# A two-group hybrid layer step on one core: features on partitions from the output projection on, the last projection as seven block products, and eight modulation columns moved into the gates

## The chip, the cores and the metric

The kernel runs on one core of one Trainium2 chip. The metric is the device time of one execution in microseconds, taken as the median of several runs. Beside it stand profiles: one execution each, recorded by the hardware profiler, in which every instruction has a start, a length and the instruction or DMA that released it. Engine names are those of the profile: PE (TensorE matmuls), PEld (its weight loads), DVE (VectorE), ACT (ScalarE), POOL (GpSimd) and SP (SyncE, which here only issues DMAs).

## The reference

One layer (DEPTH is 1) is applied to two groups of tokens: 512 sample tokens and 128 prompt tokens, 640 together, with 1024 features. Each group has its own modulation vector. The parts that the change touches are these:

```python
mod = jax.nn.silu(cvec) @ lw['w_ada'] + lw['b_ada']
sh1, sc1, g1, sh2, sc2, g2 = jnp.split(mod, 6, axis=-1)
h = rmsnorm(x, lw['norm1_g']) * (1.0 + sc1) + sh1
mix, ... = token_mixers(h, ...)          # ends: merged @ lw['w_o']
x = x + g1 * mix
h = rmsnorm(x, lw['norm2_g']) * (1.0 + sc2) + sh2
x = x + g2 * conv_ffn(h, ...)            # (silu(g) * a) @ w_down, 2816 hidden features
y = rmsnorm(x, final_norm_g)
```

`token_mixers` computes four branches from an input projection, a sigmoid gate for each branch, and `merged`, the gated sum of four branch projections. `conv_ffn` projects up to 2 x 2816 features, applies a three-tap convolution along the tokens, multiplies silu of one half by the other and projects down. Everything is fp32.

## The kernel before

**Arithmetic.** Each fp32 operand of a large product is split in two fp32r tiles, a high part (a copy, written by ACT) and a low part (the difference, written by DVE). A product is three matmul passes: high by high, high by low and low by high. Weights arrive in fp32 by DMA, issued by SP, and are split in the kernel, so every weight tile costs one copy on ACT and one subtraction on DVE. A few low parts are formed by a DMA on POOL's queue instead (`low_dma`).

**Stages, in the order of time.** Normalization, input projections and the mixers' own work (0 to about 285 us); the first gate's tiles, one after the other (285 to 355 us); the other gates as seven-product block pairs; the output projection `wo_tile` (544 to 601 us); the second normalization; the up projection, 22 pairs of hidden tiles, each pair as seven block products of 12 matmuls 128x320 per tile set (617 to 884 us); the down projection `down_tile` (869 to 1030 us); and the final normalization. In the middle stages features lie on partitions and the 640 tokens are the moving dimension, cut in two halves of 320. From the output projection on it is the other way: five tiles of 128 tokens are on partitions, and a matmul streams 512 output features.

**Output projection and second normalization.** `wo_tile` runs over two column halves and eight feature tiles. When a token tile is complete, DVE multiplies by the gate, which has been spread over partitions as a row (`gain_rows`, line 250, transposes it and a DMA broadcasts it), and adds x. `norm2` then squares with an accumulator on ACT, takes the power -0.5 on POOL (line 264), scales, turns the tile back with eight PE transposes (line 1229) and applies scale and shift (line 1240). High and low parts follow in pieces (line 1249). The matmuls of the first up products (line 1387, called the bridge below) are placed between the transposes; `operands` forms the sums and differences of the up projection's input blocks in two pieces, 192 and 128 tokens wide, while the bridge runs. The pair loop's matmuls are line 1392.

**Down projection.** For each half of 512 output columns there are 11 steps of two hidden tiles; a step has 30 matmuls 128x512, or in the second half 24 of 128x512 and 12 of 128x256 (line 1708). The activations come back from DRAM (`actd`). `down_out` (lines 1719 to 1740) multiplies by the gate row, adds x, squares, takes the power on POOL, scales on ACT and DVE, and stores. Eight modulation columns, numbers 40 to 47 (the gate g2), are computed beside this stage by `ada_cols`: each is a 512 KB load and, for each of the two groups, a multiplication with a summing output on DVE (line 223 before, 224 after).

**Order of the work.** A table of units is walked with loads four units ahead and preparation two ahead. Side work is written as generators; `start` puts one in, `tick` and `pe` advance a clock by estimated PE time, and a generator goes on when the clock has passed what it yielded. `drain` forces one to its end at that point. Within the sections where `fixed[0]` is true (the gate pairs, the up projection, and after the change the down projection), DVE, ACT and POOL follow the written order; DVE operations recorded by the helper have line 138 (137 after). Elsewhere, and on PE and SP, a list scheduler sets the order. Tiles live in regions with fixed tags (`region("X0", ...)`), so a tile's reuse waits for the readers of the one before.

## Time and profile before

| | |
|---|---|
| median of 3 runs | 1039.47 us (1039.32 to 1042.35) |
| profiled execution, its own time | 1039.43 us |
| its span, first to last instruction | 1037.7 us |
| PE busy | 1021.1 us, 98% of the span |
| DVE busy | 790.5 us, 76% |
| ACT busy | 520.6 us, 50% |
| POOL busy | 99.7 us, 10% |
| mean granted PE clock | 0.998 |

Matmuls are pipelined and overlap in the records, so the mean length of one is longer than the distance from one to the next; the distance is read from the chain of waits, where a stretch of matmuls stands with its count. An entry `[0.44 <-ACT MG L138]` behind a row says that the engine was idle 0.44 us before it and that ACT's writing of tile MG, recorded at line 138, ended the idle time. The profile's lines are shown where the prediction uses them.

### The profile page before, as it was taken

The numbers are of one execution on the slowest core, as the hardware profiler recorded it, in microseconds if no ns is written. First come the engines' busy times: TensorE is split into PE (matmuls) and PEld (weight loads), VectorE is DVE, ScalarE is ACT, GpSimd is POOL, SyncE is SP. The second block draws the span as 40 slices with busy tenths as digits, with TensorE's granted clock in tenths as the row PEclk, the third lists the DMA queues.
The fourth block names the chain that finished last, engine by engine and source line by source line (L and its number), as shares of the span: only waits on it lengthen the run. The fifth ranks groups of instructions, "written<-read, shape, count | busy, mean of one in ns | idle before, by whom it ended". The sixth has DMA issues, their size and how long they took to land. (4 is left out here: it accounts for less than half of the span.)

```text
span 1037.7 us, 18776 instructions
## 1 busy us (share of the span) xinstructions
PE 1021.1 (98%) x7648; PEld 962.1 (93%) x7648; DVE 790.5 (76%) x1271; ACT 520.6 (50%) x900; POOL 99.7 (10%) x145
## 2 busy tenths in 40 slices
PE   8999999999999999999999999999999999999997
PEld 6899989998899999999998898999999999888886
DVE  5658899789946567767768688998888887785734
ACT  6542353242333444444444377876777776632532
POOL 2000020211100000000000011211111121000201
PEclk9999999999999999999999999999999999999999
DMA  9854433544143122332178274666555569974212
GB/s 363 325 196 126 126 122 105 164 144 153 52 163 117 55 99 98 107 102 80 64 246 331 113 264 126 175 172 164 162 148 148 148 154 261 378 256 144 84 39 102
DMA packets 52759, 165.28 MB, mean 159 GB/s; under 512 B 7840, under 2 KB 14400, under 8 KB 49600
## 3 DMA queue, kind: packets, MB, share of 16 engines
q1 hardware_dynamic: 43424, 137.19, 38.7%
q0 software_dynamic: 9248, 26.89, 10.4%
q8 instruction: 60, 0.98, 0.4%
q14 instruction: 27, 0.22, 0.1%
HBM read 131.52 MB, written 21.52 MB: 147 GB/s over the span
## 5 line engine op out<-in xcount | busy, mean ns | idle before, releaser
L317 PE MATMUL g<-XH,w 128*128 128x320 f32 x832 | 200.0, 317 | 0.2 <-DVE MG L378 0.2
L317 PEld LDWEIGHTS g<-XH,w 128*128 128x128 f32 x832 | 141.9, 188 | 2.9 <-issue 2.0
L317 PE MATMUL g<-XL,w 128*128 128x320 f32 x416 | 129.0, 310 | 0.0
L317 PEld LDWEIGHTS g<-XL,w 128*128 128x128 f32 x416 | 78.3, 188 | 0.8 <-issue 0.5
L270 DVE TENSOR_TENSOR w<-raw,w 128x1024 fp32r<-128x1024 f32 x34 | 41.5, 1222 | 18.3 <-ACT w L269 17.6
L1708 PE MATMUL g<-w,XH 128*128 128x512 f32 (+1 forms) x216 | 47.5, 372 | 0.0
L269 ACT ACTIVATE w<-raw 128x1024 fp32r<-128x1024 f32 x34 | 35.8, 1052 | 20.9 <-PE g L1187 10.2
L1708 PEld LDWEIGHTS g<-w,XH 128*128 128x128 f32 x216 | 38.5, 188 | 7.6 <-ACT XH L1671 0.3
L1051 PE MATMUL m<-XH,w 128*128 128x320 f32 x192 | 45.0, 309 | 0.0
L138 DVE SCALAR_TENSOR_TENSOR X<-MG,p2t,X 128x641 f32<-128x641 f32 x44 | 38.9, 884 | 5.7 <-ACT X L138 4.8
L282 ACT ACTIVATE w<-raw 128x1024 fp32r<-128x1024 f32 (+1 forms) x26 | 29.4, 1130 | 22.3 <-PE g L317 9.5
L138 DVE SCALAR_TENSOR_TENSOR X<-X,p2t,X 128x641 f32<-128x641 f32 x44 | 38.9, 884 | 1.9 <-ACT X L138 1.0
L1708 PE MATMUL m<-w,XH 128*128 128x512 f32 (+1 forms) x180 | 40.2, 368 | 0.0
L1708 PE MATMUL g<-w,XL 128*128 128x512 f32 (+1 forms) x180 | 40.0, 373 | 0.0
L1392 PE MATMUL g<-XL,C 128*128 128x320 f32 x240 | 38.6, 310 | 0.4 <-ACT MG L138 0.4
L1392 PE MATMUL g<-XL,w 128*128 128x320 f32 x240 | 38.7, 310 | 0.0
L1708 PEld LDWEIGHTS g<-w,XL 128*128 128x128 f32 x180 | 32.2, 188 | 6.8 <-DVE dt L1719 0.6
L283 DVE TENSOR_TENSOR w<-raw,w 128x1024 fp32r<-128x1024 f32 (+1 forms) x26 | 33.9, 1302 | 4.2 <-ACT w L282 4.0
L1392 PEld LDWEIGHTS g<-XL,C 128*128 128x128 f32 x240 | 35.9, 188 | 1.1 <-ACT MG L138 1.1
L1392 PEld LDWEIGHTS g<-XL,w 128*128 128x128 f32 x240 | 36.0, 188 | 0.5 <-ACT MG L138 0.3
L1708 PEld LDWEIGHTS m<-w,XH 128*128 128x128 f32 x180 | 31.3, 189 | 5.3
L1708 PE MATMUL m<-w,XL 128*128 128x512 f32 (+1 forms) x150 | 33.2, 368 | 0.0
(541 smaller groups left out, 2701.2 us busy)
## 6 DMA issues: line engine op xcount, KB each, us to landing
raw<-in_w_up_dram SPq DMA_DIRECT2D x32, 512.0 KB, 4.9
raw<-in_w_gp_dram SPq DMA_DIRECT2D x18, 640.0 KB, 3.8
raw<-in_w_down_dram SPq DMA_DIRECT2D x22, 512.0 KB, 4.0
raw<-in_w_in_dram SPq DMA_DIRECT2D x19, 512.0 KB, 4.0
H<-in_w_adt_dram SPq DMA_DIRECT2D x16, 512.0 KB, 4.2
actd<-X POOLq DMA_DIRECT2D x22, 320.5 KB, 5.3
X<-in_w_adt_dram SPq DMA_DIRECT2D x10, 512.0 KB, 4.0
raw<-in_w_gate_dram SPq DMA_DIRECT2D x8, 640.0 KB, 3.9
```

The source lines that it names most:

```text
L138: r = f(*args, **kw)
L269: act(w[0], raw, AF.Copy)
L270: vec.tensor_tensor(w[1], raw, w[0].bitcast(F32), ALU.subtract)
L282: act(w[:, 0], raw, AF.Copy)
L283: low = lambda: vec.tensor_tensor(w[:, 1], raw, w[:, 0].bitcast(F32), ALU.subtract)
L317: mm(o, w[:, h, k0 + k, :], r(k)[:, s], start=(k == 0 and i == 0), stop=(k == kt - 1 and i == 2))
L1051: mm(o, w[:, k, :], x[:, k, :], start=(first and k == 0 and j == 0), stop=(k == 3 and j == 2), skip_group_check=True)
L1392: mm(o, w[:, k, :], x[:, k, :], start=(first and k == 0 and j == 0), stop=(k == 3 and j == 2), skip_group_check=True)
L1708: mm(acc[nh][t + c0 // 256][:, 0:c1 - c0], sl[k][hx][:, t * P:(t + 1) * P], w[:, hw, k, c0:c1], start=(kk_ == 0 and k == 0 and i == 0), st ...
```

## The change

1. **Features on partitions to the end.** x is kept transposed (`x_t`, a new input layout). The output projection has eight column blocks of 128 features by two token halves of 320: 384 matmuls 128x320 (`wo_mm`). The gate is now a scalar per partition (`add_out`). The second normalization squares on ACT, adds the squares of the eight feature tiles on DVE, sums over partitions by a product with ones (`stats_a`), takes the power for three token blocks on POOL, and spreads the result over partitions by a second product (`stats_c`). The 40 transposes and the gate rows go. `operands` forms all nine sums, differences and low parts at the full width of 320, behind the statistics of the second token half.
2. **Down projection as seven block products.** The 22 hidden tiles are cut in two halves of 11, the output columns in two halves of 512 and the tokens in two halves of 320. Products run in the order 1, 5, 6, 4, 7, 2, 3, each in six groups of two hidden tiles (the last of one), 924 matmuls 128x320 in all (`group_mm`, line 1797). Sums of weight blocks are formed in place by accumulating DMAs on POOL's queue, sums and differences of activations by DVE (`prep_x`). `ended` adds a product's four outputs to x. One token half is normalized in place with features on partitions; the other is turned by 24 transposes (line 1834) and normalized with tokens on partitions. The two output halves are put together on the host.
3. **Columns 40 to 47 in the gates.** `ada_cols` for them is started when the first branch's input projections end, and is drained at the fifth tile of the first gate.

The core of the diff:

```diff
@@ ada_cols, gate_tile
+                start(ada_cols(range(40, 48), None, col_home, HD[4]))
+        if (bi, n) == (0, 4):
+            drain(lambda: "ada47" in R)
-        start(ada_cols(range(40, 48), "MG1", lambda f: region("H", [P, D]) if f % 2 else down_home(), 5))
@@ output projection
+    def add_out(ps, n, c, g, eng=None):
+        x = x2s(n, c)
+        for (t0, t1, v) in pieces(c):
+            (eng or vec).scalar_tensor_tensor(x[:, t0:t1], ps[:, t0:t1], gcol[:, g, v, n % 8:n % 8 + 1], x[:, t0:t1],
+                                              ALU.mult, ALU.add)
...
+    def stats_a(c, m):
+        for j, t in enumerate((0, P, HC - P)):
+            mm(m[:, 2 * j:2 * j + 2], axs[0][:, c, t:t + P], ones[:, 0:2], start=True, stop=True)
...
+    def stats_c(dg, m):
+        for j, (t, w) in enumerate(((0, P), (P, P), (2 * P, HC - 2 * P))):
+            mm(m[:, t:t + w], onesf, dg[:, j, P - w:P], start=True, stop=True)
...
+    def wo_mm(o, w, c, ks, first, last):
+        for k in ks:
+            for i, (hw, hx) in enumerate(((0, 0), (0, 1), (1, 0))):
+                mm(o, w[:, hw, k, :], mh[k // 2][:, hx, k % 2, c * HC:(c + 1) * HC],
+                   start=(first and k == ks[0] and i == 0), stop=(last and k == ks[-1] and i == 2))
+            tick(0.44)
@@ up_all, operands
+            if p_ == 0:
+                stats_a(1, g[0][:, 1])
+                dg = stats_b(1, g[0][:, 1])
+            if p_ == 1:
+                stats_c(dg, g[1][:, 1])
+                for q in range(2):
+                    normed(1, q, g[1][:, 1])
+                shifted(1, 0, False)
+                shifted(1, 1, True)
...
+        operands()
@@ down projection
+    def prep_w(i):
+        p_, g = GR[i]
+        n = many(g)
+        wr = slots.pop(("raw", i)) if p_ in (2, 3) else chain(g)
+        w = slots["w", i] = wp.tile([P, 2, 2, 512], F32R, tag="w", name=nm("w"))
+        oact(w[:, 0, 0:n], wr, AF.Copy)
+        ovec.tensor_tensor(w[:, 1, 0:n], wr, w[:, 0, 0:n].bitcast(F32), ALU.subtract)
+        if p_ in CHAIN:
+            opool.dma_start(flat2(wr), flat2(wblock(CHAIN[p_], g)), accum_op=ALU.add)
...
+    def prep_x(i):
...
+        if p_ == 5:
+            ovec.tensor_tensor(x, a21, a22, ALU.subtract)
+            ovec.tensor_tensor(a21, a11, a21, ALU.subtract)
+        elif p_ == 6:
+            ovec.scalar_tensor_tensor(x, a21, -1.0, a22, ALU.mult, ALU.subtract)
+        elif p_ == 7:
+            ovec.tensor_tensor(a22, a22, a21, ALU.add)
+        elif p_ == 3:
+            ovec.tensor_tensor(a12, a12, a22, ALU.subtract)
...
+    def group_mm(o, i, js):
+        for kk in range(many(g)):
+            k = 2 * g + kk
+            for j in js:
+                for q, (h, x) in enumerate(((0, 0), (0, 1), (1, 0))):
+                    mm(o[j], w[:, h, kk, j * P:(j + 1) * P], s[:, x, kk, :], ...)
```

Three places show how the order moves. In the rows, a name is tile, buffer number and version; the shape is the output's.

DVE at the start of the up projection, before: `X0` and `XL1` hold the normalized blocks, `X1` the sums, `B`, `A`, `D` the operands' high and low parts.

```order
L1249 TENSOR_TENSOR XL0_557_6178<-X0_566_6274,XL0_557_6178 128x4x128
L138 TENSOR_TENSOR X1_591_6511<-X0_566_6274 128x4x192
L138 TENSOR_TENSOR X1_591_6511<-X1_591_6511,XL1_559_6180 128x4x192
L138 TENSOR_TENSOR X0_566_6274<-XL1_559_6180,X0_566_6274 128x4x192
L138 TENSOR_TENSOR X1_591_6511<-X0_566_6274 128x4x128
L138 TENSOR_TENSOR MG1_585_6453<-m_587_6463,s1_590_6508 128x320
L1249 TENSOR_TENSOR XL0_557_6178<-X0_566_6274,XL0_557_6178 128x4x128
L138 TENSOR_TENSOR B_593_6513<-X1_591_6511,B_593_6513 128x4x192
L138 TENSOR_TENSOR A_592_6512<-X1_591_6511,A_592_6512 128x4x192
```

The same place after the change, from the scaling by the second half's statistics (`X1` by the broadcast in `g`) to the pair's weight lows:

```order
L137 TENSOR_TENSOR X1_578_6343<-X1_578_6343,g_602_6587 128x1280
...
L137 TENSOR_TENSOR X0_616_6738<-X1_578_6343 128x1280
L137 TENSOR_TENSOR X0_616_6738<-X0_616_6738,XL1_577_6337 128x1280
L137 TENSOR_TENSOR B_619_6741<-X0_616_6738,B_619_6741 128x1280
L137 TENSOR_TENSOR X1_578_6343<-XL1_577_6337,X1_578_6343 128x1280
L137 TENSOR_TENSOR A_618_6740<-X0_616_6738,A_618_6740 128x1280
L137 TENSOR_TENSOR D_620_6742<-X1_578_6343,D_620_6742 128x1280
L137 TENSOR_TENSOR X0_616_6738<-XL1_577_6337,X0_616_6738 128x1280
L137 TENSOR_TENSOR XL0_617_6739<-X1_578_6343,XL0_617_6739 128x1280
L137 TENSOR_TENSOR XL1_621_6755<-X0_616_6738,XL1_621_6755 128x1280
L137 TENSOR_TENSOR MG1_606_6622<-m_612_6685,s1_613_6698 128x320
L137 TENSOR_TENSOR w_624_6788<-F_600_6581,w_624_6788 128x1024
```

Two pieces of 192 and 128 have become one operation each, and the first of them stands behind the scaling by the second half's statistics; the pair's weight lows are last.

DVE in the first gate's tiles, before: MG0 are the merges, the 128x1280 rows the operands of the block pairs.

```order
L915 TENSOR_TENSOR MG0_324_3529<-g_342_3716,gt_341_3714 128x640
L965 TENSOR_TENSOR C_336_3647<-B_337_3648,C_336_3647 128x1280
L283 TENSOR_TENSOR w_346_3734<-raw_328_3554,w_346_3734 128x1280
L967 TENSOR_TENSOR C_336_3647<-C_336_3647 128x1280
L977 TENSOR_TENSOR X0_343_3723<-C_336_3647,X0_343_3723 128x1280
```

After, the stretch ahead of the fifth merge (MG1):

```order
L224 SCALAR_TENSOR_TENSOR junk_365_3857,ar_366_3858<-MG1_315_3431,S0_89_1054 128x1024
...
L224 SCALAR_TENSOR_TENSOR MG1_315_3431,ar_366_3858<-MG1_315_3431,S0_89_1054 128x1024
L962 TENSOR_TENSOR X0_370_3903<-C_342_3662,X0_370_3903 128x1280
...
L224 SCALAR_TENSOR_TENSOR junk_368_3897,ar_369_3898<-MG1_315_3431,S0_89_1054 128x1024
L962 TENSOR_TENSOR F_372_3905<-B_343_3663,F_372_3905 128x1280
L224 SCALAR_TENSOR_TENSOR MG1_315_3431,ar_369_3898<-MG1_315_3431,S0_89_1054 128x1024
...
L905 TENSOR_TENSOR MG1_373_3907<-g_374_3908,gt_367_3895 128x640
```

The sixteen column operations stand between the merges and the operands' operations, the last one just ahead of the fifth merge, whose tile takes over the region of the columns' data.

PE where the down projection begins, after the change: `g_780` is the up projection's last pair, `m_796` to `m_799` the four output blocks of the first product.

```order
L1437 MATMUL g_780_9288<-D_620_6742,w_779_9253 128x320
L1797 MATMUL m_796_9479<-XH_788_9411,w_787_9407 128x320
...
L1797 MATMUL m_798_9481<-XH_788_9411,w_787_9407 128x320 x2
L1437 MATMUL g_780_9288<-XL0_617_6739,w_779_9253 128x320 x12
...
L1797 MATMUL m_799_9482<-XH_788_9411,w_787_9407 128x320 x3
L1437 MATMUL g_780_9288<-XL1_621_6755,w_779_9253 128x320 x12
L1797 MATMUL m_796_9479<-XH_788_9411,w_789_9422 128x320 x3
...
L1797 MATMUL m_796_9479<-XH_788_9411,w_802_9509 128x320
```

The first group (weights `w_787`) now stands around the last pair's two last products, the second group directly behind; `w_802` is the fourth group's.

More of the change, by code (lines that the diff above doesn't have):

```diff
@@ L953, in g_operands @@
         yield 8
+        while "ada47" not in R:
+            yield 1
         (a11, a12), (a21, a22) = [[x[:, h] for h in range(2)] for x in f]
@@ L1253, in tile_step, with pieces @@
[L1253 to L1257 removed]
+    st2 = const.tile([P, 4, 4], F32, name="st2")
+    axs = [None]
+    x2d = dram.tile([2, P, 4, T], F32, name="x2d")
+    KO = ((0, 1, 4, 5), (2, 3, 6, 7))
+    HOLD = 5
+    def pieces(c):
+        return ((0, HC, 0),) if c == 0 else ((0, TS - HC, 0), (TS - HC, HC, 1))
@@ new lines, in normed, with shifted @@
+    def normed(c, q, m):
+        f = hh[c][:, q]
+        ovec.tensor_tensor(f, f, m[:, 0:HC].unsqueeze(1).to_broadcast([P, 4, HC]), ALU.mult)
+    def shifted(c, q, on_vec):
+        f = hh[c][:, q]
+        for k in range(4):
+            for (t0, t1, v) in pieces(c):
+                x, sh = f[:, k, t0:t1], modt[:, 24 + 4 * q + k, v:v + 1]
+                if on_vec:
+                    ovec.tensor_scalar(x, x, sh, None, ALU.add)
+                else:
+                    oact(x, x, AF.Identity, bias=sh)
@@ L1261, in tile_step @@
+    for n in range(8):
+        plain(lambda n=n: feat(a["w_o"][n]), lambda w, n=n: wo_tile(n, w))
     actd = dram.tile([NPAIR, P, T + 1], F32, name="actd")
@@ L1556, in up_pair @@
             prod(b1, p_, 7, False)
[L1558 to L1571 removed]
+        if p_ == NPAIR - 1:
+            down_start(1)
@@ new lines, in backs, with chain, wblock @@
+    def backs(o, h, c, eng=nc.sync):
+        k = 0
+        while k < 11:
+            k1 = min(11, k + 8 - (12 * o + k) % 8)
+            back(o, h, c, k, k1, eng)
+            k = k1
+    def chain(g):
+        tag, n, at = (("S0", 4, 2 * g), ("S0", 4, 2 * g), ("H", 2, 0), ("F", 5, 0), ("F", 5, 2), ("F", 5, 4))[g]
+        if "w" + tag not in dn:
+            dn["w" + tag] = region(tag, [P, n, 512])
+        return dn["w" + tag][:, at:at + many(g)]
+    def wblock(b, g):
+        return a["w_down"][b[0], b[1]][:, 2 * g:2 * g + many(g)]
```

663 lines of the change are left out of this document (363 added, 300 removed).

## The prediction

> **What bounds the kernel now.** I read the page's busy shares and slices first, for what is busy in every stage.
>
> ```profile
> PE 1021.1 (98%) x7648; PEld 962.1 (93%) x7648; DVE 790.5 (76%) x1271; ACT 520.6 (50%) x900; POOL 99.7 (10%) x145
> PE   8999999999999999999999999999999999999997
> PEclk9999999999999999999999999999999999999999
> ```
>
> TensorE is busy in 98% of the span at the full granted clock. So the time is a sum of matmul pitches plus a few stalls, and a change is worth what it takes out of, or puts between, matmuls. The pitches stand in the chain of waits (start us, length, what); a stretch without a stall divided by its count gives one pitch.
>
> ```profile
> 668.91 10.56 PE g L1392 x72
> ...
> 904.89 1.36 PE m L1708 x6
> 906.25 5.44 PE g L1708 x24
> ...
> 972.18 2.07 PE g L1708 x12
> 974.25 4.83 PE m L1708 x24
> ```
>
> A 128x320 matmul takes 10.56/72 = 0.1467 us, a 128x512 one 5.44/24 = 0.2267. A down-projection step of 30 takes 6.80; the steps of the second half, with 256-wide pieces, 6.90. Next, the busy time by stage (busy us and instructions of PE, PEld, DVE, ACT, POOL; clock; DMA share; GB/s): gates' first tiles (two rows), up projection, its hand-over to the down projection, both down halves, and the end.
>
> ```profile
> 284.00:327.00 43.00, 42.88 (x301) 40.34 (x300) 28.34 (x38) 18.04 (x22) 0.00 (x0) 1.00 0.44 150
> 327.00:336.00 9.00, 9.00 (x63) 9.00 (x62) 2.32 (x2) 2.07 (x2) 0.00 (x0) 1.00 0.27 89
> 632.00:870.00 238.00, 238.00 (x1620) 237.53 (x1619) 213.84 (x315) 172.69 (x296) 43.67 (x58) 1.00 0.61 162
> 870.00:893.00 23.00, 23.00 (x122) 19.71 (x121) 17.98 (x24) 14.93 (x24) 3.12 (x5) 1.00 1.03 345
> 893.00:950.00 57.00, 57.00 (x254) 47.10 (x253) 45.19 (x69) 23.08 (x29) 0.00 (x0) 1.00 0.73 248
> 950.00:1030.00 80.00, 80.00 (x414) 68.32 (x412) 42.53 (x58) 28.45 (x48) 10.14 (x9) 1.00 0.23 79
> 1030.00:1038.00 8.00, 0.13 (x2) 0.00 (x0) 1.92 (x6) 1.69 (x6) 0.55 (x1) 0.68 0.32 132
> ```
>
> VectorE has little room in the up projection (213.84 of 238) and no stall comes of it there; it has most room in the second down half. The only stalls that this change touches are behind the output projection, in the timeline of PE (the bracket is the idle time before the row and its releaser):
>
> ```profile
> 616.75 0.31 PE L1392 MATMUL g<-B,E 128*128 128x320 f32 x1
> ...
> 625.57 1.59 PE L1392 MATMUL g<-A,w 128*128 128x320 f32 x9 [1.15 <-DVE w L138]
> ...
> 631.36 1.92 PE L1392 MATMUL g<-B,w 128*128 128x320 f32 x12
> ```
>
> From 616.75 to 631.36 72 matmuls run; at the pitch they need 10.56 us, so 4.05 us are lost there.
>
> **The change part by part.** The profiled execution takes 1039.43 us for a span of 1037.7; that is the median of the runs, 1039.47, within 0.04, so I add the terms to 1039.4.
>
> *Down projection.* Before: 11 x 6.80 + 11 x 6.90 = 150.7 us. After: 6 groups a product, five of 24 and one of 12 matmuls, so 132 x 7 = 924 of 128x320, 135.5 us. Term: **-15.2**, if PE stays the bound. The Trainium skill (TensorE: Matmul & The Clock Gate, "Back-to-back issue gap") gives a warm gap of N/2.4 + 2.5 ns, so 135.8 and 215.8 ns; by it the term would be 924 x 0.1358 - (594 x 0.2158 + 132 x 0.1092) = -17.1. The trace has 10.8 ns more in every matmul, which tells against a change to more and narrower ones, and its pitch stands.
>
> *Does VectorE keep up there?* Prices:
>
> ```profile
> L138 DVE TENSOR_TENSOR w<-raw,w 128x1024 fp32r<-128x1024 f32 x15 | 18.3, 1222 | 2.7 <-ACT w L138 2.7
> L138 DVE TENSOR_TENSOR MG<-MG,ga 128x640 f32<-128x640 f32 x12 | 9.9, 825 | 0.4
> L138 DVE TENSOR_TENSOR gb<-m,gb 128x320 f32<-128x320 f32 x24 | 11.6, 484 | 0.0
> L138 POOL DMA_DIRECT2D w<-F x11 | 9.5, 862 | 103.4 <-ACT w L138 90.5 <-PE g L1392 12.9
> w<-F POOLq DMA_DIRECT2D x11, 256.0 KB, 3.2
> ```
>
> Per product 5.5 weight lows (1.22) are 6.7 us. Over the stage that is 47; some 19 input lows that are not formed by DMA (0.82) 16; block differences 12 + 6 + 6 + 6 pieces of 0.82, less the half-wide last ones, 23; 36 output additions, 20 of 0.48 and 16 in two pieces that I put at 0.65, 20; sums of squares and final scaling 16. About 122 us of 135.5, or 112 where successive ones overlap as they do in the windows. That is no more than the up projection's 90%. The tightest is product 5: 6.7 + 9 for two differences a group + 2 lows 1.6 + 2.2 of outputs = 19.5 against 132 x 0.1467 = 19.4. The weight sums are DMA accumulates on POOL, 0.86 to issue and 3.2 to land, a product (19.4) ahead of their use: no term.
>
> *Up to down.* Before, PE passed from the up to the down projection without a stall. Now group 0 is placed ahead of the last two products of the last pair, but group 3's weights stand on VectorE behind that pair's taps and gate, while DMA is full (share 1.03). With product 5's tight start I take **+2** (an estimate): 0 if PE's lead holds, +6 if a back-load lands like the slow one instead of the quick one.
>
> ```profile
> E<-actd SPq DMA_DIRECT2D x1, 1024.0 KB, 5.1
> A<-actd SPq DMA_DIRECT2D x1, 1024.0 KB, 11.2
> ```
>
> *Output projection and norm.* 240 x 0.2267 = 54.4 before, 384 x 0.1467 = 56.3 after: +1.9. Forty transposes go; two sums against ones, and eight transposes:
>
> ```profile
> 100.86 0.28 PE L418 MATMUL m<-heads,E 128*128 128x2 f32 x2
> ...
> 601.95 1.04 PE L1229 MATMUL m<-cst,C 128*128 128x128 f32 x8
> 602.74 0.40 PE L1387 MATMUL g<-XH,MG 128*128 128x320 f32 x1
> ```
>
> The last row starts 0.79 behind the transposes, so 40 are 3.95. The added fp32 sums (128x2) take about 0.14 each, three 0.42, and the broadcast, 320 wide, about 0.56 by the transposes' 0.1 for 128 at double passes; twice over, 2.0. Together **-0.1**. The down stage gets one more such set, **+1.0**, and some 24 transposes, of which those between matmuls cost **+0.4**. Two dropped transposes of gate rows, 0.1 each, give **-0.2**.
>
> *Start of the up projection.* The token-wise norm let operands be formed in pieces of 192 and 128; now all nine follow the statistics of the second half at full width. Prices:
>
> ```profile
> 622.88 1.49 DVE L138 TENSOR_TENSOR XL<-X,XL 128x1280 fp32r<-128x1280 f32 x1 [1.99 <-ACT XL L138]
> 624.29 1.82 DVE L138 TENSOR_TENSOR w<-F,w 128x1024 fp32r<-128x1024 f32 x2
> L138 DVE TENSOR_TENSOR X<-g,X 128x192 f32<-128x192 f32 x20 | 7.0, 352 | 0.0
> ```
>
> One starts 1.41 after the other. From the broadcast on, VectorE does two scalings (2.8), eight shifts (2.6), one pair's product (0.5), two differences (2.8) and B's low (1.4): 10.1 us. PE has 56 bridge matmuls, 8.2. Stall 1.9. A's low is 2.8 behind B's against 12 matmuls, 1.8: 1.0. Four more lows and differences (5.6), 0.5 and the pair's weight lows (1.8) are 7.9 against some 30 matmuls, 4.4: 3.5. Half a microsecond to one for the first half's lows. Sum 7 against the 4.05 now: **+3.0**. Bounds: -2 if the second half's statistics come earlier than the written order says; +11 below, as a rival.
>
> *Gates.* Eight columns, two STTs each:
>
> ```profile
> L223 DVE SCALAR_TENSOR_TENSOR H<-H,S 128x1024 f32<-128x1024 f32 x12 | 14.6, 1218 | 0.1
> 308.38 1.49 DVE L961 TENSOR_TENSOR B<-B 128x1280 f32<-128x1280 f32 x1 [4.73 <-DMA B<-hdr]
> 311.37 1.49 DVE L963 TENSOR_TENSOR B<-C,B 128x1280 f32<-128x1280 f32 x1 [1.49 <-DMA C<-hdr]
> ```
>
> 16 x 1.22 = 19.5 us must end before the fifth merge; VectorE is idle 43.0 - 28.3 + 9.0 - 2.3 = 21.4 us up to the merge at 336. It fits by 2 us, unless the waits for hdr (6.2) cannot be filled, since the columns' eight loads now stand in SP's queue beside hdr's. Queued behind a waiting STT are the merges, and PE waits for those by its PSUM. Between 0 and +6.2, taken **+1**: the columns come free one by one into such waits.
>
> *Tail.*
>
> ```profile
> 1028.53 1.60 PE L1708 MATMUL m<-w,XH 128*128 128x256 f32 x12
> 1032.32 0.55 POOL L1735 TENSOR_TENSOR st<-st,neghalf 128x1 f32<-128x1 f32 x1 [3.02 <-DVE st L1731]
> 1032.90 0.72 ACT L1737 ACTIVATE G<-G,st 128x512 f32<-128x512 f32 x1 [0.86 <-POOL st L1735]
> 1033.75 0.33 SPq L1740 DMA_DIRECT2D out_dram<-G  x1
> L264 POOL TENSOR_TENSOR dss<-dss,neghalf 128x5 f32<-128x5 f32 x1 | 1.8, 1755 | 92.2 <-DVE dss L263 92.2
> ```
>
> Now 7.6 us from the last matmul (1030.1) to the end, 3.95 of them behind the DMA's issue. After: addition and square, 1.7; six sums 0.8; a 128x3 power, between 0.55 and 1.76, 1.2; three scalings a side, 2.0; hand-overs 0.5; DMA 3.9. That is 10.1: **+2.5** (0 to +4).
>
> Sum: -15.2 - 0.1 + 1.0 + 0.4 - 0.2 + 3.0 + 2 + 1 + 2.5 = -5.6, **1033.8 us**. A measurement of this kernel tells about 0.3% (3.1 us) from no change, so 1036.3 to 1042.6 counts as the same.
>
> **Rivals.** *All covered* (18%): up-start, up-to-down and gates cost nothing more (0 instead of 6): 1027.8. For it: in 238 us of up projection VectorE is 90% busy without one PE stall. Against: the chains above are longer than their cover.
>
> *VectorE sets the down stage's pace* (16%): if waits for ScalarE's copies hold it to the first down half's share, 45.19 of 57 or 0.79, its 112 us are 142 instead of 135.5, or +6.3: 1040.1, no change. For it: 19.5 against 19.4 in product 5. Against: lows and sums may run ahead in product 4, which has little.
>
> *Clock* (4%, at the same time): PE's granted clock is 0.68 in the last window, after PE went idle; if it falls for some 3 us in each of three stalls, about 1.5 us each are lost, +4.5: 1038.3. The Trainium skill (TensorE: Matmul & The Clock Gate, "Part 1: The HAM clock gate") says that an idle window of about 3.4 us halves the clock; the trace agrees in that last window, and the stalls quoted above stay under 2 us each. Of mine only w's, 3.5, comes up to such a window.
>
> *The operand chain runs in series* (13%): one place, the start of the up projection. A full-width high copy takes ScalarE 1.3 us:
>
> ```profile
> L282 ACT ACTIVATE w<-raw 128x1280 fp32r<-128x1280 f32 x8 | 10.2, 1272 | 8.0 <-PE g L317 8.0
> ```
>
> If each of nine high copies on ScalarE waits for VectorE, as XL waited 1.99 above, and each low for its copy, 9 x 1.3 = 11.7 us join the 7: 1045.5, slower. It decides from 8.8 us beyond my term on. For it: that [1.99 <-ACT XL] row. Against: ScalarE is at half load, and copies can follow their operand while the next is formed.
>
> **How the numbers follow.** Forecast 49%, all covered 18, pace 16, clock 4, series 13. The forecast's own range by its bounds is 1029 to 1038; all covered reaches to 1026, series starts at 1043. Range 1026 to 1042.5. Faster: 18 + most of the forecast 44 + some of clock and pace 4 = 0.66; same 0.21; slower 0.13.
>
> **What would show it.** In the changed profile: a down stage of about 924 pitches, 135 to 139 us; bracketed stalls for B, A and w at the start of the up projection summing to about 7; merges of the gates no later than before; some 10 us after the last matmul. Wrong would be: stalls spread through the products (pace), a granted clock under 1 at a hand-over, or a gap over 10 us ahead of the first pairs.

## The result, and the profile after

The changed kernel takes 1071.24 us, the median of four runs (1062.48 to 1073.08), against 1040.91 (1039.32 to 1042.48) for the kernel before in the same session: a ratio of 1.0275 with a 95% interval of 1.0214 to 1.0335. The change makes the kernel slower; 1033.8 with a range of 1026 to 1042.5 had been predicted. The profiled execution took 1072.0 us for a span of 1070.2, so 32.5 us of span are to be found against the 1037.7 before.

The page first (PE and DMA by slices, in tenths, and the software queue's packets, MB and share):

```profile
PE   8999999999999999999999989999999999587996
...
DMA  9844433472283223323269526566655589799794
...
q0 software_dynamic: 15968, 49.07, 20.4%
```

The same rows of the kernel before:

```profile
DMA  9854433544143122332178274666555569974212
...
q0 software_dynamic: 9248, 26.89, 10.4%
```

A slice is 26.8 us. PE has three bad ones, 5, 8 and 7 tenths, from 910 to 990 us, soon after the down projection begins. The last eight digits of the DMA row, from 856 us on, now read 8, 9, 7, 9, 9, 7, 9, 4; before they read 6, 9, 9, 7, 4, 2, 1, 2.

Common points of the two programs split the 32.5 us. They are the second sigmoid of the first gate (the last point at which both agree: 299.10 before, 299.07 after), the first matmul of the gate pairs (353.46 and 358.35), of the output projection (543.64 and 548.55) and of the bridge (600.92 and 606.46), the row `g<-B,w` that ends the start of the up projection (631.36 and 642.87), the end of the last down matmul (1030.1 and 1058.4) and the end.

| stretch | before, us | after, us | difference | predicted |
|---|---|---|---|---|
| to the gate pairs | 54.4 | 59.3 | +4.9 | +0.8 (gates, gate rows) |
| gate pairs | 190.2 | 190.2 | 0.0 | 0 |
| output projection, norm up to the bridge | 57.3 | 57.9 | +0.6 | +0.5 |
| bridge to `g<-B,w` | 30.4 | 36.4 | +6.0 | +2.4 |
| up and down projection | 398.7 | 415.5 | +16.8 | -11.8 |
| tail | 7.6 | 11.8 | +4.2 | +2.5 |

The predicted terms are put where the work stands. Of the 40 transposes that go, 24 stood ahead of the bridge and 16 in its stretch, and one set of the new sums (1.0) comes in each; so the -0.1 and the +3.0 of the prediction are +0.5 and +2.4 here. (The two gate rows, 0.1 each, stand near 136 and 947 us; both are counted in the first line.)

So 28.6 us of the error lie in one row, and 9.5 in the others together.

**The down stage.** PE's timeline there (start, length, what, count; in brackets the idle time before and its releaser), the four longest of ten stalls that together take 24.3 us:

```profile
920.92 0.90 PE L1797 MATMUL g<-XL,w 128*128 128x320 f32 x2 [9.10 <-ACT w L137]
...
933.56 3.94 PE L1797 MATMUL g<-XH,w 128*128 128x320 f32 x25 [2.91 <-DMA XH<-x]
...
953.89 7.49 PE L1797 MATMUL m<-XL,w 128*128 128x320 f32 x48 [3.21 <-DMA XL<-x]
...
975.19 3.30 PE L1797 MATMUL m<-XH,w 128*128 128x320 f32 x11 [5.89 <-DMA XH<-x]
```

The first names ScalarE. ScalarE had waited for VectorE, and VectorE's own timeline names what came last:

```profile
918.32 0.82 DVE L137 TENSOR_TENSOR x<-C,A 128x640 f32<-128x640 f32 x1 [12.16 <-DMA A<-actd]
...
951.12 0.88 DVE L1164 SCALAR_TENSOR_TENSOR X<-g,gcol,X 128x320 f32<-128x320 f32 x2 [3.40 <-DMA X<-x2d]
```

`A` holds most of the third quarter of the activations (a22; eight of its eleven tiles), needed for the differences of product 5; the weights' low stands behind that operation in VectorE's queue. The chain of waits says the same without detour:

```profile
877.53 8.81 PE g L1437 x60
...
888.73 3.75 SPq L1705
...
892.53 25.61 DMA A<-actd
...
940.51 10.48 DMA X<-x2d
...
963.79 11.35 DMA XH<-x
...
998.46 19.36 PE m L1797 x132
```

Up to 975 the chain is mostly three transfers, 47 us together, and the issue of the first. SyncE issues `A` in order, behind loads that had waited for the up product whose matmuls end at 886.34. The last piece of the chain shown is PE without a break: 132 matmuls take 19.4 (0.147 each, as predicted). The windows show why transfers are slow (columns as in the prediction: busy times, clock, DMA share, GB/s):

```profile
877.00:893.00 16.00, 15.62 (x105) 15.09 (x104) 10.39 (x14) 10.33 (x18) 4.44 (x6) 1.00 0.99 285
893.00:960.00 67.00, 49.58 (x315) 47.44 (x314) 43.01 (x59) 26.91 (x38) 19.68 (x25) 0.92 0.92 209
960.00:1037.00 77.00, 70.50 (x465) 69.83 (x464) 51.75 (x81) 43.01 (x63) 18.98 (x22) 0.96 0.91 207
```

The DMA engines are over 90% busy for 160 us and move only 207 to 285 GB/s. In the windows of the kernel before, which the prediction shows, 0.73 gave 248 GB/s from 893 to 950 and 0.23 was enough from 950 on.

### The profile page after: what moved, and what is told of

Read it like the earlier page. It is cut to its first block, busy times and chain, and to the rows that moved or that the text cites. A ratio compares the mean times of both kernels' runs of the same rounds, so it can differ in the third digit from the quotient of the medians.

```text
span 1070.2 us, 19703 instructions
## 1 busy us (share of the span) xinstructions
PE 1023.8 (96%) x8020; PEld 995.4 (93%) x8020; DVE 825.6 (77%) x1343; ACT 546.1 (51%) x934; POOL 127.7 (12%) x180
## 3 DMA queue, kind: packets, MB, share of 16 engines
q0 software_dynamic: 15968, 49.07, 20.4%
q8 instruction: 63, 1.03, 0.4%
## 5 line engine op out<-in xcount | busy, mean ns | idle before, releaser
L304 PE MATMUL g<-XH,w 128*128 128x320 f32 x832 | 203.0, 320 | 2.1 <-ACT gt L892 2.1
L304 PE MATMUL g<-XL,w 128*128 128x320 f32 x416 | 130.6, 314 | 0.0
L1797 PE MATMUL m<-XH,w 128*128 128x320 f32 x264 | 42.3, 318 | 7.4 <-DMA XH<-x 5.9
L137 ACT ACTIVATE w<-F 128x512 fp32r<-128x512 f32 (+1 forms) x59 | 43.4, 774 | 11.1 <-PE g L1797 6.4
L1797 PEld LDWEIGHTS m<-XH,w 128*128 128x128 f32 x264 | 40.2, 194 | 8.5 <-DMA XH<-x 6.2
L270 DVE TENSOR_TENSOR w<-raw,w 128x1024 fp32r<-128x1024 f32 (+1 forms) x34 | 43.8, 1287 | 5.2 <-ACT w L269 5.0
L1036 PE MATMUL m<-XH,w 128*128 128x320 f32 x192 | 45.0, 309 | 0.0
L137 DVE TENSOR_TENSOR w<-raw,w 128x1024 fp32r<-128x1024 f32 (+2 forms) x39 | 38.0, 989 | 9.0 <-ACT w L137 8.6
L1797 PE MATMUL m<-XL,w 128*128 128x320 f32 x264 | 40.4, 311 | 3.8 <-DMA XL<-x 3.8
L1797 PEld LDWEIGHTS m<-XL,w 128*128 128x128 f32 x264 | 38.9, 188 | 4.5 <-DMA XL<-x 4.3
L137 DVE TENSOR_TENSOR w<-F,w 128x1024 fp32r<-128x1024 f32 (+1 forms) x37 | 35.6, 988 | 9.4 <-ACT w L137 9.2
L1437 PE MATMUL g<-XL,w 128*128 128x320 f32 x240 | 38.7, 310 | 0.0
L1797 PE MATMUL g<-XL,w 128*128 128x320 f32 x180 | 28.9, 322 | 9.5 <-ACT w L137 9.1
L1797 PE MATMUL g<-XH,w 128*128 128x320 f32 x216 | 33.6, 314 | 3.7 <-DMA XH<-x 3.7
```

The source lines that it names most:

```text
L137: r = f(*args, **kw)
L270: low = lambda: vec.tensor_tensor(w[:, 1], raw, w[:, 0].bitcast(F32), ALU.subtract)
L304: mm(o, w[:, h, k0 + k, :], r(k)[:, s], start=(k == 0 and i == 0), stop=(k == kt - 1 and i == 2))
L1036: mm(o, w[:, k, :], x[:, k, :], start=(first and k == 0 and j == 0), stop=(k == 3 and j == 2), skip_group_check=True)
L1437: mm(o, w[:, k, :], x[:, k, :], start=(first and k == 0 and j == 0), stop=(k == 3 and j == 2), skip_group_check=True)
L1797: mm(o[j], w[:, h, kk, j * P:(j + 1) * P], s[:, x, kk, :], start=(p_ in (1, 5, 4, 2, 3) and k == 0 and q == 0), stop=(k == 10 and q == 2), ...
```

## The experiments

The theory after this reading: the down stage is bound by its transfers. The change has put three things into them (additions on arrival, short rows, lows formed by DMA), and each can be taken away alone. The rivals are that one of the three is the whole cause, or that the columns or VectorE are. Ratios are to the kernel before.

**The accumulating loads made plain.**

```diff
-            opool.dma_start(flat2(wr), flat2(wblock(CHAIN[p_], g)), accum_op=ALU.add)
+            opool.dma_start(flat2(wr), flat2(wblock(CHAIN[p_], g)))
...
-            chained.append(lambda: opool.dma_start(flat2(wr), flat2(wblock((1, 1), g)), accum_op=ALU.add))
+            chained.append(lambda: opool.dma_start(flat2(wr), flat2(wblock((1, 1), g))))
```

> The changed kernel (1071 us), with the 30 accumulating loads of weight blocks on POOL's queue made plain loads of the same bytes; the weight sums are left out, everything else is as it was. Accumulate theory (transfers bound the start of the down stage, 0.9 to 1.0 DMA share from 885 to 975 us, because an accumulating load costs about twice a plain one): the load of A from actd lands some 10 us earlier than 25.6 us after its issue, the 24 us of PE stalls in the stage fall under 12, and the time falls to 1050-1058. Short-rows theory (768 and 512 byte rows of the activations' way back are what costs): stalls stay above 20, time 1066-1073. Lows theory (PE waits for input lows that a DMA forms behind POOL's queue): the 9.1 us stall shrinks little, the stalls for XH and XL stay, time 1062-1070.

Measured: 1046.95 us, ratio 1.0062 (1.0044 to 1.0080); 24.3 us below the changed kernel, and 3 us below the range of the accumulate theory, whose other signs came: the stalls sum to 6.5. DMA issues of the changed kernel (name, queue, count, size, median us from issue to landing):

```profile
S<-in_w_down_dram POOLq DMA_DIRECT2D x8, 512.0 KB, 6.9
F<-in_w_down_dram POOLq DMA_DIRECT2D x8, 512.0 KB, 8.8
...
A<-actd SPq DMA_DIRECT2D x1, 512.0 KB, 25.6
```

and of this one:

```profile
S<-in_w_down_dram POOLq DMA_DIRECT2D x8, 512.0 KB, 4.7
F<-in_w_down_dram POOLq DMA_DIRECT2D x8, 512.0 KB, 4.6
...
A<-actd SPq DMA_DIRECT2D x1, 512.0 KB, 12.8
```

The same issues with the same bytes land in 4.6 to 4.7 us instead of 6.9 to 8.8, and what stands beside them lands sooner too: `A` in half the time, the reload of x in 7.1 instead of 10.8, the plain loads into `H` in 5.5 instead of 7.6. The 9.10 stall is gone; the longest left is 1.45. The software queue's row is now

```profile
q0 software_dynamic: 15712, 49.07, 18.1%
```

so its packets' time falls from 20.4% of a span of 1070.2 to 18.1% of 1045.4, that is from 218 to 189 us of all 16 engines. The accumulating loads are 24, not the 30 of the expectation (20 of 512 KB and 4 of 256 KB), 11 MB: adding on arrival cost 29 us of all 16 engines. The packets of the two traces agree: on the software queue one of 4096 bytes takes 328 ns (median) in the changed kernel and 159 here, while those of 1280 and 2560 bytes take 121 and 215 in both. (This kernel leaves the weight sums out, so it prices the step and is no remedy.)

**The short rows.** The second token half lies in DRAM with a column between the two groups, so its reload is two DMAs with rows of 768 and 512 bytes. Here it is one with rows of 1280.

```diff
-            eng.dma_start(dst[:, :, 0:TS - HC], src[:, :, HC:TS])
-            eng.dma_start(dst[:, :, TS - HC:HC], src[:, :, TS + 1:T + 1])
+            eng.dma_start(dst, src[:, :, HC:T])
```

> The changed kernel, with the second token half of the activations fetched in one piece of 1280-byte rows in place of a 768- and a 512-byte piece (one column too early, so the gap column is taken for a token). Short-rows theory: A lands 10 us or more earlier, 1054-1062. Accumulate theory: at most 2-3 us, 1066-1072. Lows theory: no more than 3 us.

Measured: 1060.83, ratio 1.0195 (1.0170 to 1.0221), 10.4 below the changed kernel, inside the range of the short-rows theory. The 9.1 stall goes here too, because `A` is issued at 881.1 and lands 20.5 later, but stalls of 5.88, 1.94 and 4.40 behind DMA-formed lows and the rest remain. (The first down matmul starts at 880.17, so `A` is there 21.4 behind it, and was 31.9 behind it in the changed kernel. Some of the gain lies ahead of the stage, and the two intervals just overlap.)

**Low parts on VectorE.** The list of activation groups whose low part a DMA forms is emptied.

```diff
-    X_DMA = [(p_, g) for p_, gs in ((5, range(2, 6)), (6, (1, 3, 5)), (7, (1, 3)), (2, range(6)), (3, range(6)))
-             for g in gs]
+    X_DMA = []
```

> The changed kernel, with all input lows of the down stage formed by VectorE (21 more subtractions of 0.74 us, 16 us in a stage of 165) and none by DMA. Lows theory: the stalls for XH and XL, 13.4 us in all, go and the 9.1 for w stays: 1056-1062. Accumulate theory: 6.6 MB fewer bytes of accumulating DMA, so 4-8 us less: 1062-1067. Short-rows theory: no change, 1068-1074; if VectorE sets the pace, slower than 1074.

Measured: 1056.7, ratio 1.0164 (1.0148 to 1.0180), 14.5 below the changed kernel, in the range of the lows theory. As that theory said, all stalls behind `XH<-x` and `XL<-x` go and the first one stays:

```profile
915.82 0.90 PE L1796 MATMUL g<-XL,w 128*128 128x320 f32 x2 [9.34 <-ACT w L137]
```

So the two long kinds of stall have two causes: the accumulations and short rows delay `A`, and the lows formed by DMA are late in the same full engines.

**The columns left out of the gates.**

```diff
-                start(ada_cols(range(40, 48), None, col_home, HD[4]))
...
-        if (bi, n) == (0, 4):
-            drain(lambda: "ada47" in R)
```

> The changed kernel without modulation columns 40 to 47 (their loads and the sixteen operations on VectorE are left out, the second gate is set to one). If the columns cause the gates' loss: the merge of the eighth tile of the first gate starts at 354-355 as before instead of 359.2, no 2.1 us stall and no clock under 1 there, time 5 us less, 1064-1068. If it is the new order of the gates alone (regions, loads): the merge stays near 359.

Measured: 1067.06, ratio 1.0253 (1.0219 to 1.0286), 4.2 below the changed kernel. The intervals overlap, so this difference alone decides nothing; the traces do. In the timelines from the second sigmoid to the first matmul of the gate pairs, before:

```profile
299.10 0.80 ACT L904 ACTIVATE gt<-g,p1t 128x640 f32<-128x640 f32 x1 [0.23 <-PE g L317]
...
353.46 0.31 PE L1051 MATMUL m<-XH,w 128*128 128x320 f32 x1
```

after:

```profile
299.07 0.79 ACT L892 ACTIVATE gt<-g,p1t 128x640 f32<-128x640 f32 x1 [5.64 <-PE g L304]
...
358.35 0.31 PE L1036 MATMUL m<-XH,w 128*128 128x320 f32 x1
```

without columns:

```profile
300.15 0.80 ACT L893 ACTIVATE gt<-g,p1t 128x640 f32<-128x640 f32 x1 [0.37 <-PE g L306]
...
354.51 0.31 PE L1033 MATMUL m<-XH,w 128*128 128x320 f32 x1
```

That is 54.36, 59.28 and again 54.36 us: what the gates lose here is the columns' doing. It is one execution each; the other kernels with the columns lose 1.3 to 4.2 in the same place. And some 0.8 of the 4.9 is a shift, since ten small matmuls (299.11 to 299.90) that stood ahead of this sigmoid's point now stand behind it. How the columns do it stands in the changed kernel's timelines:

```profile
309.14 1.49 DVE L946 TENSOR_TENSOR B<-B 128x1280 f32<-128x1280 f32 x1 [2.41 <-DMA B<-hdr]
...
310.71 1.27 ACT L961 ACTIVATE X<-B 128x1280 fp32r<-128x1280 f32 x1 [7.62 <-DVE B L946]
311.89 0.78 ACT L892 ACTIVATE gt<-g,p1t 128x640 f32<-128x640 f32 x1
...
312.72 0.41 PE L304 MATMUL g<-XH,w 128*128 128x320 f32 x1 [2.14 <-ACT gt L892]
```

VectorE reaches the operand `B` late, between two column operations and behind a load that came late. ScalarE's copy of `B` waits for it, and the gate's sigmoid, for which everything was ready, stands behind that copy in ScalarE's order. Without the columns the sigmoid stands ahead of the copy (307.90 and 309.96 in the kernel before, 308.95 and 310.54 in this experiment). PE waits for the sigmoid to free its PSUM: 2.14 here, 0 to 1.42 in the other kernels with the columns, which have the same order. Behind the stall the clock is at 0.69 for 5.5 us:

```profile
312.50:318.00 5.50, 5.28 (x25) 5.28 (x26) 5.46 (x8) 1.33 (x2) 0.00 (x0) 0.69 0.93 285
```

**The three together, and the columns alone.** The first three edits in one kernel, and in the other the kernel before with nothing but part 3 of the change:

```diff
...
+                start(ada_cols(range(40, 48), None, col_home, HD[4]))
...
+        if (bi, n) == (0, 4):
+            drain(lambda: "ada47" in R)
...
-        start(ada_cols(range(40, 48), "MG1", lambda f: region("H", [P, D]) if f % 2 else down_home(), 5))
```

> The changed kernel with all three edits of the runs before: plain loads for the accumulating ones (weight sums left out), the second token half fetched in whole rows (gap column taken for a token), all input lows on VectorE. This is the stage with the transfers eased. If transfers are all that went wrong in the down stage: no PE stall over 2 us from 880 us on, the stage near 135.5 plus 3, time 1034-1040 (the gates' and the up-start's losses of some 6 us stay). If VectorE, now with 16 us more, is the next bound: stalls named DVE w of 5-10 us, 1041-1048.

> The kernel before with the third part of the change alone: columns 40 to 47 started behind the first branch's projections, drained at the fifth gate tile, nothing of them in the down stage. If the columns cost the gates 1-5 us, and the down stage has room for them: 1040.5-1044. If they cost the down stage as much as the gates: 1039-1040.

Measured: 1045.4, ratio 1.0048 (1.0030 to 1.0066), and 1043.77, ratio 1.0030 (1.0019 to 1.0040). With all three edits no stall of the down stage exceeds 0.60 and their sum is 4.0, but the time stays above the kernel before. The expectation of 1034 to 1040 is missed; the second, 1041 to 1048, has the number, but not its sign, waits of 5 to 10 us for VectorE. The columns alone came out as expected. The span with all three edits, 1043.6, is 5.9 longer than before. Its `g<-B,w` starts at 639.67, 8.3 later (gates 2.9, start of the up projection 4.6, output projection 0.6, rest before the gates), the stretch to the last down matmul (1031.6) is 6.8 shorter, and the tail of 12.0 is 4.4 longer. So even with its transfers eased the change would not pay, and the columns alone cost the kernel before 0.3%.

**Products 5 and 6 alone on VectorE; weight sums on GpSimd.** The first forms the lows of products 5 and 6 on VectorE and leaves those of 7, 2 and 3 to the DMA. The second does the same, loads every weight block plainly and adds it on GpSimd:

```diff
-    X_DMA = [(p_, g) for p_, gs in ((5, range(2, 6)), (6, (1, 3, 5)), (7, (1, 3)), (2, range(6)), (3, range(6)))
+    X_DMA = [(p_, g) for p_, gs in ((7, (1, 3)), (2, range(6)), (3, range(6)))
...
-            opool.dma_start(flat2(wr), flat2(wblock(CHAIN[p_], g)), accum_op=ALU.add)
+            nc.sync.dma_start(r, wblock(CHAIN.get(p_, (1, 1)), g))
+            pend.append(lambda: opool.tensor_tensor(flat2(wr), flat2(wr), flat2(r), ALU.add))
```

> The changed kernel with the seven DMA-formed lows of products 5 and 6 formed by VectorE, those of products 7, 2 and 3 still by DMA. Congestion theory (a transfer taken out of the stretch from 900 to 960 counts, one behind 975 does not): at least as fast as with all lows on VectorE, 1052-1057. If DMA-formed lows cost PE wherever they stand: 1060-1065.

> The run above, and the weight sums formed by POOL additions (about 3 us each by the 128x512 addition's 1.49, 23 of them) of plainly loaded blocks in place of accumulating DMAs: the result is the reference's. Accumulate theory: the 20 us that plain loads gave come back less what POOL's additions take from VectorE: 1038-1048. If it is POOL's queue that is late, not the DMA's bytes: 1055 or more, with stalls for w behind POOL.

Measured: 1059.33, ratio 1.0176 (1.0158 to 1.0194), and 1073.89, ratio 1.0318 (1.0303 to 1.0334). Both miss what the congestion theory gave. The first lies between its two ranges and is not told from all lows on VectorE, whose interval it overlaps; the first stall (8.7) stays in it as it does there (9.34). The second has the highest median of all, with an interval that overlaps the changed kernel's. Its groups of instructions (busy us, mean ns, idle time):

```profile
L137 POOL TENSOR_TENSOR S<-S,raw 128x1024 f32<-128x1024 f32 x8 | 22.8, 2861 | 15.5 <-DVE w L137 9.3 <-DMA S<-in_w_down_dram 5.9 <-DMA H<-in_w_down_dram 0.3
L137 DVE TENSOR_TENSOR w<-F,w 128x512 fp32r<-128x512 f32 x16 | 15.3, 957 | 0.4 <-ACT w L137 0.4
```

and one moment of it on both engines:

```profile
888.47 5.67 POOL L137 TENSOR_TENSOR S<-S,raw 128x1024 f32<-128x1024 f32 x2
...
888.85 3.02 DVE L137 TENSOR_TENSOR XH<-E,XH 128x640 fp32r<-128x640 f32 x1
891.80 3.94 DVE L137 SCALAR_TENSOR_TENSOR X<-MG,p2t,X 128x641 f32<-128x641 f32 x2
...
897.76 0.82 DVE L137 TENSOR_TENSOR XH<-E,XH 128x640 fp32r<-128x640 f32 x1 [0.49 <-ACT XH L137]
```

The same subtraction takes 3.02 us beside GpSimd's addition and 0.82 without it. PE's waits change from DMA to VectorE (5.13, 2.80 and many of 0.7 to 0.95). The Trainium skill (SBUF — State Buffer, "Who interferes with whom") says that a VectorE instruction with two SBUF inputs contends with a GpSimd instruction that reads SBUF, through a pair of ports that one of them holds for a whole instruction; this trace agrees, since the first subtraction ends about where GpSimd's first addition does.

**The whole computation with better transfers.** The activations are stored without the column between the groups (two stores a pair instead of one), so that each token half reloads as one DMA with full rows, and no low is formed by DMA in the down stage. The second kernel also issues each accumulating load three groups later.

```diff
...
-        opool.dma_start(actd[p_], up[p_, "z", 1])
+        z = up[p_, "z", 1]
+        opool.dma_start(actd[p_][:, 0:TS], z[:, 0:TS])
+        opool.dma_start(actd[p_][:, TS:T], z[:, TS + 1:T + 1])
...
+            eng.dma_start(dst, src[:, :, HC:T])
...
-            opool.dma_start(flat2(wr), flat2(wblock(CHAIN[p_], g)), accum_op=ALU.add)
+            later.append((i + 1, lambda: opool.dma_start(flat2(wr), flat2(wblock(CHAIN[p_], g)), accum_op=ALU.add)))
```

(The last two lines are the second kernel's alone; it issues from `later` when step i is reached.)

> The whole computation, with no low part of the down stage formed by DMA (VectorE forms them) and the stored activations without their gap column: each tile pair is stored by two DMAs instead of one, and every reload of a token half is then one DMA with rows of 1280 bytes. The accumulating loads stay. Congestion theory (the hand-over to the down projection waits for the stored activations, which come late because too many transfers with short rows and accumulations stand beside them): the 9 us stall behind ScalarE's copy shrinks below 3 us, the time is 1047 to 1052, and it stays above the 1045.4 of the kernel that also loaded its weight blocks plainly. Rival (the 9 us stall hangs on the accumulations alone): the stall stays at 8 to 10 us and the time at 1055 to 1058, as without the DMA-formed lows alone. Either way it should not beat the kernel before: gates, start of the up projection and tail still cost some 10 us between them.

> The same, with each accumulating load of a weight block issued three groups (about 10 us) later, still three groups ahead of its use. Congestion theory: the reloaded activations no longer share the DMA engines with six accumulations, so they land in 12 to 15 us instead of 19 to 25, and the time is 1043 to 1048, within 2 us of the kernel with plain loads (1045.4). Rival (an accumulation costs the same wherever it stands, because the stage is full of them): the same time as without the delay, within 1.5 us. A third way: the late sums now stall ScalarE's copies of product 5's weights, with stalls of 3 us and more from 905 on and a time above the undelayed one.

Measured: 1053.23, ratio 1.0117 (1.0090 to 1.0144), and 1054.27, ratio 1.0133 (1.0111 to 1.0156). The first is 18.0 below the changed kernel and 3.5 below the one with VectorE's lows alone; the time lies 1.2 above the congestion theory's range (its runs spread from 1048.29 to 1054.54), but the stall shrinks as that theory said. The longest at product 5 is now 1.63:

```profile
926.95 0.85 PE L1797 MATMUL g<-XH,w 128*128 128x320 f32 x4 [1.63 <-ACT w L137]
```

`A` is there some 20 us behind the first down matmul (issued at 888.36, landed in 19.0, first matmul at 887.83), where it had been 32 (918.1 and 886.16). With the accumulations moved back it lands in 10.3 us, and that brings nothing, which was the rival's result. PE's stalls in that kernel:

```profile
918.35 0.42 PE L1798 MATMUL g<-XH,w 128*128 128x320 f32 x1 [2.33 <-DVE XH L137]
...
970.72 0.55 PE L1798 MATMUL g<-XL,w 128*128 128x320 f32 x2 [1.51 <-ACT w L137]
```

Its DMA share is 0.77 instead of 1.00 from 870 to 900, and 1.05 instead of 0.83 from 920 to 940. The work has only moved, and the later sums, the reload of x (16.2 us instead of 9.3) and product 4's blocks meet it there. No version of the change that was run beats the kernel before.

The stage alone, from the start of `g<-B,w` to the end of the last down matmul in each profiled execution, leaves out what the gates and the clock do elsewhere:

| kernel | stage, us |
|---|---|
| before | 398.7 |
| changed | 415.5 |
| without columns in the gates | 414.8 |
| accumulating loads made plain | 393.8 |
| whole rows | 406.2 |
| lows on VectorE | 405.8 |
| the three together | 391.9 |
| lows of 5 and 6 alone on VectorE | 405.4 |
| weight sums on GpSimd | 420.6 |
| stored without the column, no DMA lows | 396.0 |
| the same, sums later | 400.7 |

The single gains of 21.7, 9.3 and 9.7 don't add: together they are 23.6. Plain loads alone bring nearly all of it, so the accumulations are the largest part, and the other two matter where the engines are already full. The kernel stored without the column computes the whole and is 2.7 us shorter than before in this stage; what it loses, it loses elsewhere.

## Why the prediction was wrong, point by point

**Where it was right.** The matmul pitch held: 924 matmuls at 0.147, 19.36 us per 132 where nothing stops PE. Without long stalls the -15.2 shows up as a gain of 6.8; of the 8.4 between, 4.0 are short stalls, 1.4 were predicted for statistics and transposes, and 3.0 are not assigned. The output projection (+0.6 against +0.5 by place) and the 0 of the gate pairs stand.

**The step that failed: "The weight sums are DMA accumulates on POOL ... no term."** The row of 3.2 us from issue to landing is itself an accumulating one, `w<-F`, 256 KB added from SBUF to SBUF. But 3.2 is a median from the up projection, where the DMA engines have room. At the hand-over of the kernel before, where the share is 1.03, the same issue took twice as long:

```profile
w<-F POOLq DMA_DIRECT2D x1, 256.0 KB, 6.4
```

and with 512 KB in the changed kernel it is 6.9 to 8.8. The test was whether each transfer lands a product ahead of its own use, while the question was what it does to the others: `A` lands in 25.6 us. What it takes from them could be worked out from the same row's packets: 2048 bytes in 178 ns, so 11 MB, 5632 packets, are some 63 us of all 16 engines (an estimate from the trace of the kernel before), and 63 is what the accumulating packets took in the changed kernel, against 34 as plain ones. Undoing this one step, in the kernel that leaves the sums out, brings 24.3 of the 30.3 us. The part "Does VectorE keep up there?" counted an engine's operations, and its 112 to 122 us of 135.5 were not the bound; it left out the DMA engines, whose share was 1.03 and 0.73 in the two windows quoted ahead of it, while the change takes the software queue from 26.89 to 49.07 MB.

**The hand-over, "+2 ... 0 if PE's lead holds, +6 if a back-load lands like the slow one instead of the quick one".** The right place and the right kind of trouble, bounded by a row of 11.2 us from a stage with fewer transfers. In its place: stalls of 24.3 us, 9.1 of them at the first use of `A`, and some 4 us of matmuls at half clock behind them (11 matmuls in 3.30 us in the row at 975.19, for 1.6 at the pitch). Against -11.8 predicted for the whole stretch, +16.8 came; stalls beyond the 2 make 22.3 of the 28.6, the clock about 4, and 2 are not assigned.

**Start of the up projection, "+3.0".** The stretch took +6.0, where +2.4 was predicted by place. The size of the stalls was nearly right: by the prediction's own measure, matmuls less their pitch, the 72 matmuls take 19.40 instead of 10.56, and with 0.97 ahead of `XH` that is 9.8 lost, against the 7 predicted. In the kernel with whole rows it is 7.8 at a full clock. The two longest stalls of the timeline:

```profile
624.96 1.87 PE L1437 MATMUL g<-B,E 128*128 128x320 f32 x11 [1.18 <-DVE B L137]
...
632.28 0.90 PE L1437 MATMUL g<-D,E 128*128 128x320 f32 x2 [2.64 <-ACT MG L137]
```

With 0.97 before `XH`, 0.79 before `A` and 0.44 behind the last of these the brackets sum to 6.0, where they were 2.4 in the kernel before: +3.6. The sums against ones and the broadcast (1.3) come for 16 transposes (1.6): -0.3. That leaves 2.7, and most of it is the clock: from 620 to 645 it is 0.86 in this execution, and 1.00 in the one with whole rows, whose stalls there are the same (0.97, 1.19, 0.78, 2.64, 0.44, and one of 0.42 more). There the stretch takes 34.4 us, here 36.4. The clock was a rival with 4%, because only a stall of 3.5 was thought to come near an idle window.

The mechanism was right in part. `B` came late from VectorE as forecast (1.2, for 1.9), but the longest stall, put at 3.5 on the pair's weight lows, is 2.64 behind ScalarE's queue:

```profile
630.63 1.27 ACT L137 ACTIVATE XL<-X 128x1280 fp32r<-128x1280 f32 x1 [1.79 <-DVE X L137]
631.81 0.42 ACT L137 ACTIVATE MG<-g 128x320 f32<-128x320 f32 x1
```

PE's product for `MG` was through at 629.64, when PE went idle. ScalarE's copy of it, which frees the PSUM, stands behind the copy of `XL`, and that one waits for VectorE. It is the pattern of the gates. The rival of a chain in series (+14.7) did not come.

**Gates, "+1", between 0 and 6.2.** +4.9 in this execution and +1.3 to +4.2 in the other kernels with the same code there (+3.1 in the kernel before with the columns). The prediction named the waiting multiplications' followers, the merges; it was ScalarE's queue, with the sigmoid behind the copy of `B`, that let the wait through. The upper bound held.

**Tail, +2.5 against +4.2.** The changed kernel's end:

```profile
1062.31 0.16 DVE L137 TENSOR_SCALAR st<-g 128x3 f32<-128x3 f32 x1 [1.39 <-PE g L1908]
1062.55 0.88 POOL L137 TENSOR_TENSOR st<-st,neghalf 128x3 f32<-128x3 f32 x1 [10.04 <-DVE st L137]
1063.47 2.06 DVE L137 TENSOR_SCALAR X<-m,st 128x512 f32<-128x512 f32 x3 [1.00 <-POOL st L137]
1064.18 3.06 SPq L1915 DMA_DIRECT2D out_dram<-X  x6
```

The power took 0.88, under the 1.2 assumed, and scaling 2.0 was right. But the sums end only at 1062.3, 3.9 after the last matmul where 2.5 had been worked out: VectorE first works off the blocks before the last one, whose own addition starts at 1059.95, 1.55 after the matmul. And from the scaling to the end it is 6.7 instead of 5.9, since six stores are issued until 1067.2.

**The rivals.** "VectorE sets the down stage's pace" was the nearest in sign and had the wrong engine: VectorE's share is 43.01 of 67 in the bad window. Its waits came from DMA. None of the rivals had a transfer as the bound of a stage, though the share was in the quoted rows.

## What to carry to other kernels

Where a change adds transfers to a stage, add up the time of all 16 DMA engines there, share times length plus what is new, as is done for an engine; a load that has "a product of lead" is late all the same when the sum exceeds the stage. A time from issue to landing is not carried from a stage where the engines have room to one where they are full (3.2 and 6.4 us for the same issue here). And an operand that a wait delays should be looked for in every in-order queue that it passes: here a waiting copy on ScalarE kept a ready sigmoid behind it in the gates, and the copy of a ready product at the start of the up projection.

## What the runs showed that was not expected

- Accumulating a weight block on arrival: 6.9 to 8.8 us for 512 KB against 4.6 to 4.7 for the same issue without the addition, and 29 us of all 16 engines over 11 MB; a packet of 4096 bytes takes 328 ns instead of 159.
- Half clock behind short stalls, in some executions only. Windows of the start of the up projection, changed kernel:

```profile
620.00:645.00 25.00, 19.95 (x112) 18.91 (x111) 21.36 (x25) 14.12 (x21) 2.10 (x9) 0.86 0.23 59
```

  and the kernel with whole rows, with the same stalls to 0.02 us:

```profile
620.00:645.00 25.00, 19.69 (x126) 18.59 (x127) 22.88 (x29) 17.63 (x27) 2.59 (x10) 1.00 0.25 64
```

  The Trainium skill (TensorE: Matmul & The Clock Gate, "Part 1: The HAM clock gate") speaks of an idle window of about 3.4 us that runs freely, so that its phase varies from run to run. The varying agrees. The longest stall here is 2.64 us, shorter than that window, and the clock still fell; behind stalls of 2.1 us (gates) and 2.6 us up to 2 us were lost so.
- GpSimd's additions made a subtraction of 0.82 us on VectorE take 3.0. Beside the accumulating DMAs nothing of the kind shows (`w<-F,w 128x512` takes 685 ns on the mean in the changed kernel, 957 beside GpSimd); they delay other DMAs instead.
